# One transformer block on one core: conv taps and norm sums shared out anew, three norms' roots made with tokens on partitions, GpSimd closing part of the last norm

## The chip, the cores and the metric

The kernel runs as one program on one core of a Trainium2 chip. The metric is the device time of one execution in microseconds (us). The core has five instruction streams: TensorE (PE, with its weight loads shown apart as PEld), VectorE (DVE), ScalarE (ACT), GpSimd (POOL) and SyncE (SP), which here only issues DMAs.

## The reference

One block (DEPTH is 1) is applied to 1024 latent tokens of 1024 channels, all in float32. Context tokens and the DeltaNet layers of the full model don't enter at this depth. What is computed:

```python
mod = silu(c) @ w_mod + b_mod                 # six vectors: sh1 s1 g1 sh2 s2 g2
h = rms_norm(x, norm1_g) * (1 + s1) + sh1
u = h @ w_pw1 + b_pw1                         # 1024 -> 2048
u = a * sigmoid(gate)                         # the two halves of u
u = dwconv(u, w_dw) + b_dw                    # 31 taps, inside 16 segments of 64 tokens
u = silu(layer_norm(u, ln_g, ln_b))
x = x + g1 * (u @ w_pw2 + b_pw2)
h = rms_norm(x, norm2_g) * (1 + s2) + sh2
x = x + g2 * (relu(h @ w1) ** 2 @ w2)         # 1024 -> 4096 -> 1024
out = rms_norm(x, final_g)
```

## The kernel before

**Layout.** Channels lie on the 128 partitions in 8 chunks, tokens along the free dimension in two blocks of 512, A (`b` = 0) and B (`b` = 1). A tile `small` is 128x512, `big` 128x1024, `bank` one PSUM bank of 128x512.

**Products.** Every float32 product is three matmuls (`product`, lines 417 to 419): each operand is a rounded high part (an ACT cast) and the low remainder (a subtraction, line 366, on DVE or POOL), and hi·hi, hi·lo and lo·hi are summed. The second MLP product saves one block product in eight by sums and differences of blocks (`mlp_joint`, 7 of its groups `g`; matmuls at lines 838 to 840; the sums S of weights and T of hidden values are wide 128x1024 operations, also line 366). The eighth group, `mlp_apart`, forms its blocks directly, first for A, then for B.

**Stages.** Head: modulation vectors (`mod_chunk`, on DVE at line 516, or a POOL multiply at line 524 with an ACT sum at line 529) and the first norm of A. Then pointwise 1 with its gate, for A and B in the order of `PW1_ORDER`. Then the depthwise conv of A, its layer norm and pointwise 2, the second norm of A, and the first MLP product of A in 32 units (`up_first`). Block B's conv, layer norm, pointwise 2 and second norm are given out over those units: conv chunk c at unit `CONV_B[c]`, the layer norm at `LN_B`, pointwise 2 at `PW2_B`. Then the MLP of B, the eight groups, and the last norm (`finish`, line 912, and the output DMAs, line 919).

**Conv taps.** Of the 31 taps of a chunk one or two start the sums on ACT (line 598); `PE_TAPS` are matmuls with a diagonal matrix (line 616); `POOL_TAPS` are an ACT multiply (line 646) and a POOL add (line 651); the rest are DVE multiply-adds (line 661) into a PSUM bank. Lines 671 and 680 on DVE add the parts.

**Norm sums.** `Mean` takes eight chunks. The first 8 - `direct` are added up on an engine (line 366, POOL unless said), and the sum and each direct chunk go into PE (`feed`, line 438) as the moving operand of a matmul with a 128x128 matrix of 1/1024. This leaves the mean of each token in every partition of a bank. `rstd_of` makes the root over 128x512 on ACT (line 479) and its reciprocal on DVE (line 481). In a layer norm the mean is subtracted (line 695, DVE), squares are made (line 469, ACT), summed, and the result multiplied in (line 707, DVE), then silu (line 712), cast (line 359) and low part (line 366).

**Order.** All instructions are put in order before anything runs, by a list scheduler in the kernel (`Plan.run`): each operation has a cost in a table, an engine and a priority (the number given by `plan.at` plus its turn); on each engine the ready operation of smallest priority goes next, if tiles are free (`SLOTS`; `KEEP` holds back some for what comes soon, `CAPS` limits kinds of tiles). In this plan a POOL operation and a DVE operation marked `port` don't overlap. The order is then fixed, and an instruction that waits holds up everything behind it on its engine.

## Time and profile before

| | us |
|---|---|
| three runs | 1048.54, 1049.9, 1049.7 (median 1049.7) |
| profiled execution: its time / its span | 1048.54 / 1046.8 |
| PE busy | 979.6 (94%) |
| PE weight loads busy | 785.8 (75%) |
| DVE busy | 737.9 (70%) |
| POOL busy | 555.9 (53%) |
| ACT busy | 513.4 (49%) |
| first product starts / output DMAs of B are issued from | 23.25 / 1039.07 |
| mean granted TensorE clock | 0.982 |

A row of the timeline gives the start, the time, the engine, the line, the operation with its output and inputs and the number of instructions put together; in brackets the idle time just before it and who ended it. A group row gives the total busy time, the mean of one in ns, and the idle time before the group with its releasers. Single stages differ much from the average: DVE's busy share is near the whole for a long stretch and a third elsewhere.

### The profile page before, as it was taken

The page shows a single profiled execution, that of the slowest core. Times are in us where ns is not written, and L with a number is a line of the kernel's source. Part 1 is how long each engine was busy: PE and PEld are TensorE (multiplying, and loading weights), DVE is VectorE, ACT ScalarE, POOL GpSimd, SP SyncE. Part 2 cuts the span into 40 slices and gives each one's busy share as a digit, 9 for nine tenths or more (in the row PEclk, how much of TensorE's full clock was granted, in tenths as well). Part 3 has the DMA queues.
Part 4 walks back from the last instruction along what each step waited for, and adds up shares of the span by engine and source line. Part 5 has one row for each costly group of instructions (what it writes and reads, how often), then busy time and mean ns, then how long its engine had stood idle before and what let it go on. Part 6 is the DMA issues. An engine that isn't in the chain of part 4 may idle for free. (4 is left out here: it accounts for less than half of the span.)

```text
span 1046.8 us, 11616 instructions
## 1 busy us (share of the span) xinstructions
PE 979.6 (94%) x4164; PEld 785.8 (75%) x4164; DVE 737.9 (70%) x957; ACT 513.4 (49%) x757; POOL 555.9 (53%) x341
## 2 busy tenths in 40 slices
PE   1999999939999998999999999999999999999994
PEld 0877777618788886788788888888888888878783
DVE  6989999995399994623374666776767677575465
ACT  4476445787567873773363424343242524333222
POOL 0045678998978998661344244345344443632322
PEclk9999999969999998999999999999999999999998
DMA  9910213735415553554070411414131231303012
GB/s 359 402 72 1 81 41 124 259 110 175 178 66 186 171 178 105 181 182 159 21 280 2 138 64 44 138 61 141 40 122 59 77 119 47 121 1 121 0 50 111
DMA packets 52521, 125.26 MB, mean 120 GB/s; under 512 B 4464, under 2 KB 21104, under 8 KB 52464
## 3 DMA queue, kind: packets, MB, share of 16 engines
q1 hardware_dynamic: 52464, 124.53, 33.9%
q8 instruction: 32, 0.52, 0.2%
q14 instruction: 25, 0.20, 0.1%
HBM read 111.93 MB, written 12.58 MB: 119 GB/s over the span
## 5 line engine op out<-in xcount | busy, mean ns | idle before, releaser
L366 POOL TENSOR_TENSOR big<-big 128x1024 fp32r<-128x1024 f32 (+1 forms) x133 | 325.5, 2459 | 339.1 <-DVE big L366 218.6
L417 PE MATMUL bank<-big 128*128 128x512 f32 x896 | 358.2, 400 | 18.6 <-ACT big L359 11.1
L419 PE MATMUL bank<-big 128*128 128x512 f32 x896 | 351.1, 392 | 1.8 <-DVE big L366 1.8
L418 PE MATMUL bank<-big 128*128 128x512 f32 x896 | 351.6, 392 | 0.4 <-DVE big L501 0.3
L727 DVE SCALAR_TENSOR_TENSOR small<-bank,mod,small 128x512 f32<-128x512 f32 x228 | 170.5, 750 | 197.5 <-PE bank L840 144.4
L366 DVE TENSOR_TENSOR big<-big 128x1024 fp32r<-128x1024 f32 (+2 forms) x137 | 189.7, 1412 | 36.9 <-ACT big L379 18.5
L417 PEld LDWEIGHTS bank<-big 128*128 128x128 f32 x896 | 169.8, 190 | 59.8 <-ACT big L359 11.9
L661 DVE SCALAR_TENSOR_TENSOR bank<-small,vec,bank 128x472 f32<-128x472 f32 (+9 forms) x320 | 198.5, 694 | 3.1 <-ACT bank L598 2.2
L418 PEld LDWEIGHTS bank<-big 128*128 128x128 f32 x896 | 169.8, 189 | 40.6 <-issue 3.5
L419 PEld LDWEIGHTS bank<-big 128*128 128x128 f32 x896 | 169.7, 189 | 37.7 <-DVE big L366 2.2
L839 PE MATMUL bank<-big 128*128 128x512 f32 x456 | 178.2, 391 | 2.5 <-DVE big L366 2.4
L838 PE MATMUL bank<-big 128*128 128x512 f32 x456 | 177.9, 390 | 0.0
L840 PE MATMUL bank<-big 128*128 128x512 f32 x456 | 177.4, 389 | 0.0
L798 ACT CAST big<-big 128x1024 fp32r<-128x1024 f32 x106 | 106.1, 1045 | 93.1 <-POOL big L366 40.5
L651 POOL TENSOR_TENSOR small<-small 128x392 f32<-128x392 f32 (+3 forms) x104 | 110.0, 1075 | 28.0 <-ACT small L646 15.5
L379 ACT CAST big<-big 128x1024 fp32r<-128x1024 f32 x92 | 95.1, 1041 | 21.1 <-PE bank L840 11.4
L366 POOL TENSOR_TENSOR small<-small 128x512 f32<-128x512 f32 x44 | 57.0, 1295 | 90.8 <-ACT small L469 59.4
L839 PEld LDWEIGHTS bank<-big 128*128 128x128 f32 x456 | 85.6, 188 | 23.3 <-DVE big L366 5.4
L838 PEld LDWEIGHTS bank<-big 128*128 128x128 f32 x456 | 85.6, 188 | 18.2 <-issue 0.2
L840 PEld LDWEIGHTS bank<-big 128*128 128x128 f32 x456 | 85.6, 188 | 17.4
L786 ACT ACTIVATE small<-bank 128x512 f32<-128x512 f32 x32 | 19.2, 599 | 154.3 <-PE bank L419 154.3
L469 ACT ACTIVATE small<-small 128x512 f32<-128x512 f32 x64 | 38.3, 624 | 87.8 <-DVE small L727 85.2
(54 smaller groups left out, 628.0 us busy)
## 6 DMA issues: line engine op xcount, KB each, us to landing
big<-in_w SPq DMA_DIRECT2D x96, 512.0 KB, 3.8
big<-in_wmod SPq DMA_DIRECT2D x48, 512.0 KB, 5.3
big<-in_wpw SPq DMA_DIRECT2D x28, 512.0 KB, 5.0
hidden<-small SPq DMA_DIRECT2D x32, 256.0 KB, 2.4
big<-hidden SPq DMA_DIRECT2D x16, 512.0 KB, 4.6
small<-in_xA SPq DMA_DIRECT2D x16, 256.0 KB, 4.5
big<-in_wfirst SPq DMA_DIRECT2D x8, 512.0 KB, 10.2
small<-in_xB SPq DMA_DIRECT2D x16, 256.0 KB, 7.3
```

What stands on the lines that cost most here:

```text
L366: lambda: eng_of[o.eng].tensor_tensor(out=out(), in0=a(), in1=b(), op=op), r, w, part=part, port=port,
L379: plan.op("act", c_act(D), lambda: act.copy(t(wh), t(raw)), [raw], [wh], also=[wl])
L417: pe.matmul(o, wh, hi(a)[:, s], start=first, stop=False)
L418: pe.matmul(o, wh, lo(a)[:, s], start=False, stop=False)
L419: pe.matmul(o, wl, hi(a)[:, s], start=False, stop=last)
L651: return pool.tensor_tensor(out=dst, in0=dst, in1=seg(t(m))[:, :, tt], op=ALU.add)
L661: dve.scalar_tensor_tensor(out=dst, in0=src, scalar=w, in1=dst, op0=ALU.mult, op1=ALU.add)
L727: lambda s=s, p=p: dve.scalar_tensor_tensor(out=t(x)[:, s], in0=cut(s, p), scalar=scale.t, in1=t(x)[:, s], op0=ALU.mult, op1=ALU.add,),
L798: plan.op("act", c_act(D), lambda: act.copy(t(h), t(x)), [x], [h], also=[l])
L838: pe.matmul(t(p), t(wh)[:, cs], t(hh)[:, ns], start=first and k == 0, stop=False, skip_group_check=not first)
L839: pe.matmul(t(p), t(wh)[:, cs], t(hl)[:, ns], start=False, stop=False, skip_group_check=not first)
L840: pe.matmul(t(p), t(wl)[:, cs], t(hh)[:, ns], start=False, stop=k == 1, skip_group_check=not first)
```

## The change

- **Taps**: `POOL_TAPS` goes from 6 per chunk of A and 7 per chunk of B to uneven lists (46 and 62 in all, before 48 and 56). `PE_TAPS` of A goes from 32 to 25. What is left falls to DVE: 161 instead of 152 for A, 162 instead of 168 for B.
- **Order of stages**: pointwise 1 of B's chunks 0 and 1 comes third and fourth; the conv chunks of B start at units 0, 3, ..., 21 instead of 0, 2, ..., 14; its layer norm and pointwise 2 at unit 22 instead of 16 and 18.
- **Low parts and block sums**: B's first MLP product has its weights' low parts on POOL instead of DVE. In a joint group, three of the four S sums go from POOL to DVE, three of seven weight low parts from POOL to DVE and three of seven hidden low parts from DVE to POOL: DVE has 14 wide operations instead of 15, POOL 12 instead of 11.
- **Norm sums**: the conv mean of A feeds two chunks directly instead of one; A's layer norm feeds all eight squares into PE instead of five (no POOL adds); B's layer norm and second norm feed only the full sum.
- **Turned roots** (`TURNED`: first norm of A, second norm of B, last norm of B): the squares' chunk becomes the stationary operand and one column of the 1/1024 matrix the moving one, four 128x1 matmuls per feed (new line 451). The mean then has the tokens on the partitions, as 128x4. Root (506) and reciprocal (508) work on 128x4. A DVE operation (512) spreads the result over a 128x512 tile of diagonals, and one matmul with the 1/1024 matrix (521) brings it into all partitions. In the head an ACT copy (526) brings it to SBUF.
- **B's first norm** (`H1B_POOL`): ACT adds the shift in place, and casts in a second pass; the low part is a POOL subtraction instead of a DVE operation.
- **Last norm of B** (`FIN_POOL` = 3): for three chunks ACT multiplies by `final_g` ahead of time (963), copies the reciprocal root to SBUF (968), and POOL multiplies; DVE does the other five.
- **Scheduler**: `KEEP` 6 and 4 become 2 and 3; `CAPS` of tap tiles 3 becomes 4, of wave tiles 12 becomes 14. The identity matrix is loaded before `vec` instead of after the head.

New line numbers of what stays: 366 is 373, 438 is 446, 479 and 481 are 499 and 501, 661 is 713, 695 is 747, 707 is 759, 727 is 779, 912 is 976.

```diff
-POOL_TAPS = ((6,) * KC, (7,) * KC)
+POOL_TAPS = ((5, 8, 5, 10, 5, 4, 7, 2), (10, 7, 5, 7, 8, 7, 9, 9))
 PW1_ORDER = (
-    (0, 4), (0, 5), (0, 6), (0, 7), (1, 4), (1, 5), (1, 6), (1, 7), (1, 0), (1, 1),
+    (0, 4), (0, 5), (1, 0), (1, 1), (0, 6),
+    (0, 7), (1, 4), (1, 5), (1, 6), (1, 7),
 )
-CONV_B = (0, 2, 4, 6, 8, 10, 12, 14)
-LN_B, PW2_B = 16, 18
-PE_TAPS = ((4,) * KC, (0,) * KC)
+CONV_B = (0, 3, 6, 9, 12, 15, 18, 21)
+LN_B, PW2_B = 22, 22
+PE_TAPS = ((4, 2, 4, 4, 2, 2, 2, 5), (0, 0, 0, 0, 0, 0, 0, 0))
-UP_LO = ("pool", "dve")
-S_ENG, T_ENG = ("pool",) * 4, ("dve",) * 4
+UP_LO = ("pool", "pool")
+S_ENG, T_ENG = ("dve", "dve", "pool", "dve"), ("dve", "dve", "dve", "dve")
-WLO_ENG, HLO_ENG = ("pool",) * 7, ("dve",) * 7
+WLO_ENG, HLO_ENG = ("pool", "pool", "dve", "pool", "dve", "dve", "pool"), ("dve", "pool", "dve", "pool", "dve", "pool", "dve")
+CM = (2, 1)
+HEAD_DIRECT, LNA, LNB, N2B, FA = 0, 8, 0, 0, 1
+TURNED = (True, False, False, False, True, True)
+H1B_POOL = True
+FIN_POOL = 3
-KEEP = {"big": 6, "small": 4}
+KEEP = {"big": 2, "small": 3}
-CAPS = {"raw": 4, "head": 7, "w": 8, "tmp": 6, "tap": 3, "taps": 4, "acc": 8, "wave": 12}
+CAPS = {"raw": 4, "head": 7, "w": 8, "tmp": 6, "tap": 4, "taps": 4, "acc": 8, "wave": 14}
...
+            def emit_turned():
+                ((_, p),) = self.acc
+                for q in range(QT):
+                    pe.matmul(
+                        t(p)[:, q : q + 1], t(x)[:, q * P : (q + 1) * P], ones.t[:, 0:1],
+                        start=first and q == 0, stop=last, skip_group_check=True,
+                    )
...
+        root = Buf(None, None, const.tile([P, QT], F32, name="root"))
...
+            lambda: act.activation(root.t, t(p)[:, 0:QT], AF.Sqrt, bias=eps.t[:, 0:1]), [p, eps], [root], "sqrt",
...
+        plan.op("dve", 100, lambda: dve.reciprocal(root.t, root.t), [root], [root])
+        spread = small(mean.b)
...
+            lambda: dve.scalar_tensor_tensor(
+                out=t(spread).rearrange("p (q n) -> p q n", q=QT),
+                in0=ident.t.unsqueeze(1).to_broadcast([P, QT, P]), scalar=float(D),
+                in1=root.t.unsqueeze(2).to_broadcast([P, QT, P]), op0=ALU.mult, op1=ALU.mult,
+            ),
...
+            lambda: pe.matmul(t(p), ones.t, t(spread), start=True, stop=True), [ones, spread], [p],
...
+        if eng == "pool":
+            plan.op(
+                "act", c_act(TB[b], 1),
+                lambda: act.activation(t(y), t(y), AF.Identity, bias=shift.t), [y, shift], [y],
+            )
+            split_pair(b, "pool", out, y)
+            return out
...
-    vA = layer_norm(0, 5)
+    vA = layer_norm(0, LNA)
...
+            if j >= KC - n:
+                binary("pool", TB[b], ALU.mult, lambda x=x: t(x), lambda x=x: t(x), lambda: t(r), [x, r], [x])
```

**How the order moves, at two places.** First DVE at A's layer norm, from the middle of the stretch between the subtractions (695 or 747) and the reciprocal of the root. The `bank<-small,vec,bank` rows are taps of block B's first chunks, `sc` and `g1b` are columns of the modulation. Before:

```order
L1013 TENSOR_SCALAR g1b<-mod,vec 128x1
L661 SCALAR_TENSOR_TENSOR bank<-small,vec,bank 128x8x53
L661 SCALAR_TENSOR_TENSOR bank<-small,vec,bank 128x8x54 x2
L661 SCALAR_TENSOR_TENSOR bank<-small,vec,bank 128x8x55
L539 TENSOR_SCALAR sc_88<-mod,vec 128x1
L661 SCALAR_TENSOR_TENSOR bank<-small,vec,bank 128x8x55
L661 SCALAR_TENSOR_TENSOR bank<-small,vec,bank 128x8x56 x2
L661 SCALAR_TENSOR_TENSOR bank<-small,vec,bank 128x8x57 x2
L661 SCALAR_TENSOR_TENSOR bank<-small,vec,bank 128x8x58
L481 RECIPROCAL bank<-bank 128x512
L707 TENSOR_TENSOR small<-small,bank 128x512 x8
```

After, from the subtractions on:

```order
L747 TENSOR_TENSOR small<-small,bank 128x512 x8
L1077 TENSOR_SCALAR g1b<-mod,vec 128x1
L713 SCALAR_TENSOR_TENSOR bank<-small,vec,bank 128x8x59 x2
L713 SCALAR_TENSOR_TENSOR bank<-small,vec,bank 128x8x60
L591 TENSOR_SCALAR sc_88<-mod,vec 128x1
L713 SCALAR_TENSOR_TENSOR bank<-small,vec,bank 128x8x60
L713 SCALAR_TENSOR_TENSOR bank<-small,vec,bank 128x8x61 x2
L713 SCALAR_TENSOR_TENSOR bank<-small,vec,bank 128x8x62 x2
L501 RECIPROCAL bank<-bank 128x512
L759 TENSOR_TENSOR small<-small,bank 128x512 x7
```

Eight taps stand between the last subtraction and the reciprocal now; before it was 19, of which the fence shows the last ten.

Second, the end of the program on DVE, from the last norm of A. Line 727 (now 779) adds products into the residual, 912 (now 976) multiplies a chunk of the output. Before:

```order
L481 RECIPROCAL bank<-bank 128x512
L912 SCALAR_TENSOR_TENSOR small<-small,vec,bank 128x512 x8
L727 SCALAR_TENSOR_TENSOR small<-bank,mod,small 128x512 x8
L481 RECIPROCAL bank<-bank 128x512
L912 SCALAR_TENSOR_TENSOR small<-small,vec,bank 128x512 x8
```

and now:

```order
L501 RECIPROCAL bank<-bank 128x512
L976 SCALAR_TENSOR_TENSOR small<-small,vec,bank 128x512 x8
L779 SCALAR_TENSOR_TENSOR small<-bank,mod,small 128x512 x8
L508 RECIPROCAL root<-root 128x4
L512 SCALAR_TENSOR_TENSOR small<-ident,root 128x512
L976 SCALAR_TENSOR_TENSOR small<-small,vec,bank 128x512 x5
```

and on PE after the last product, now (before, two 128x512 matmuls of line 438 stood there):

```order
L890 MATMUL bank<-big 128x512
L891 MATMUL bank<-big 128x512
L892 MATMUL bank<-big 128x512
L451 MATMUL bank<-ones,small 128x1 x8
L521 MATMUL bank<-small,ones 128x512
```

The 128x512 reciprocal of B's last norm has gone, a small one and the spreading operation stand in its place, three of the eight closing multiplies have left DVE, and PE has eight 128x1 matmuls and one 128x512 in place of two 128x512.

More of the change, by code (lines that the diff above doesn't have):

```diff
@@ L71 @@
 class Op:
-    __slots__ = ("eng", "costs", "emit", "prio", "table", "deps", "bufs", "left", "ready", "end", "after", "lag", "port")
+    __slots__ = ("eng", "costs", "emit", "prio", "turn", "table", "deps", "bufs", "left", "ready", "end", "after", "lag", "port")
 class Plan:
@@ L128, in run @@
         events, seq, order = [], 0, []
-        waiting = sorted(self.ops, key=lambda o: o.prio, reverse=True)
+        waiting = sorted(self.ops, key=lambda o: o.turn, reverse=True)
         def push(o):
@@ L156, in run @@
                 waiting.pop()
-            near = waiting[-1].prio + NEAR if waiting else 0
+            near = waiting[-1].turn + NEAR if waiting else 0
             for e in engines:
@@ L176, in run @@
                                 caps[b.cap] = caps.get(b.cap, 0) + 1
-                    kept = KEEP if o.prio > near else {}
+                    kept = KEEP if o.turn > near else {}
                     if any(free[s] < n + kept.get(s, 0) for s, n in need.items()) or any(
@@ L475, in rstd_of @@
         ((_, p),) = mean.acc
-        r = p if in_bank else small(mean.b)
+        if not mean.turned:
+            r = p if in_bank else small(mean.b)
+            plan.op(
+                "act", c_act(TB[mean.b]),
+                lambda: act.activation(t(r), t(p), AF.Sqrt, bias=eps.t[:, 0:1]), [p, eps], [r], "sqrt",
+            )
+            plan.op("dve", 6.4 * TB[mean.b], lambda: dve.reciprocal(t(r), t(r)), [r], [r])
+            return r
+        root = Buf(None, None, const.tile([P, QT], F32, name="root"))
         plan.op(
-            "act", c_act(TB[mean.b]),
-            lambda: act.activation(t(r), t(p), AF.Sqrt, bias=eps.t[:, 0:1]), [p, eps], [r], "sqrt",
-        )
-        plan.op("dve", 6.4 * TB[mean.b], lambda: dve.reciprocal(t(r), t(r)), [r], [r])
+            "act", 200,
+            lambda: act.activation(root.t, t(p)[:, 0:QT], AF.Sqrt, bias=eps.t[:, 0:1]), [p, eps], [root], "sqrt",
+        )
+        plan.op("dve", 100, lambda: dve.reciprocal(root.t, root.t), [root], [root])
+        spread = small(mean.b)
+        plan.op(
+            "dve", c_stt(TB[mean.b]),
+            lambda: dve.scalar_tensor_tensor(
[3 more added lines that the diff above has]
+            ),
+            [ident, root], [spread], port=True,
+        )
+        plan.op(
+            "pe", 1.67 * TB[mean.b],
+            lambda: pe.matmul(t(p), ones.t, t(spread), start=True, stop=True), [ones, spread], [p],
+        )
+        if in_bank:
+            return p
+        r = small(mean.b)
+        plan.op("act", c_act(TB[mean.b]), lambda: act.copy(t(r), t(p)), [p], [r])
         return r
@@ L906, in finish @@
     def finish(b, xl, ms):
+        n = FIN_POOL if b else 0
+        for j in range(KC - n, KC):
+            plan.op(
+                "act", c_act(TB[b], 1),
+                lambda x=xl[j], j=j: act.activation(t(x), t(x), AF.Copy, scale=col(C_FG, j)), [xl[j], vec], [xl[j]],
+            )
         rstd = rstd_of(ms)
+        if n:
+            r = small(b)
+            plan.op("act", c_act(TB[b]), lambda: act.copy(t(r), t(rstd)), [rstd], [r])
         for j in range(KC):
             x = xl[j]
-            plan.op(
-                "dve", c_stt(TB[b]),
-                lambda x=x, j=j: dve.scalar_tensor_tensor(
-                    out=t(x), in0=t(x), scalar=col(C_FG, j), in1=t(rstd),
-                    op0=ALU.mult, op1=ALU.mult,
-                ),
-                [x, rstd, vec], [x], port=rstd.size != "bank",
-            )
+            if j >= KC - n:
+                binary("pool", TB[b], ALU.mult, lambda x=x: t(x), lambda x=x: t(x), lambda: t(r), [x, r], [x])
+            else:
+                plan.op(
+                    "dve", c_stt(TB[b]),
+                    lambda x=x, j=j: dve.scalar_tensor_tensor(
+                        out=t(x), in0=t(x), scalar=col(C_FG, j), in1=t(rstd),
+                        op0=ALU.mult, op1=ALU.mult,
+                    ),
+                    [x, rstd, vec], [x], port=rstd.size != "bank",
+                )
             plan.op(
@@ L946, in trunk @@
     xs0 = load_x(0)
+    load(ident, eye, P)
     load(vec, vecs, NVEC)
-    ms = Mean(0, 0, "dve")
+    ms = Mean(0, HEAD_DIRECT, "dve", TURNED[0])
     for k in range(KC):
@@ L970, in trunk @@
     plan.at(1010)
-    load(ident, eye, P, [h1[0][5]])
     xs1 = load_x(1, [h1[0][5]])
@@ L980, in trunk @@
         h1[1].append(
-            modulated(1, xs1[k], r1, sc1[k], mod[SH1][k], True)
+            modulated(1, xs1[k], r1, sc1[k], mod[SH1][k], True, "pool" if H1B_POOL else "dve")
         )
@@ L1059, in trunk @@
         up_part(0, i)
-    sums = Mean(0, 1), Mean(1, 1)
+    sums = Mean(0, FA), Mean(1, 1, turned=TURNED[5])
     for g in range(NQ):
```

26 lines of the change are left out of this document (16 added, 10 removed).

## The prediction

> **What bounds the kernel now.** I read PE's waits first, since PE is busy for 94% of the span. They come to some 39 us, nearly all of it waits for other engines' norm work. They are listed as engine, line, what was waited for, us in total, times, longest.
>
> ```profile
> PE bank L438 <- POOL small L366: 16.9, 5, 8.5
> PE bank L438 <- DVE small L366: 14.5, 1, 14.5
> PE bank L417 <- ACT big L359: 11.1, 1, 11.1
> PE bank L417 <- ACT big L497: 6.7, 1, 6.7
> PE bank L839 <- DVE big L366: 2.4, 5, 1.8
> PE bank L419 <- DVE big L366: 1.8, 1, 1.8
> ```
>
> The head has 14.5 + 6.7; A's layer norm 8.5 + 11.1; B's layer norm most of the rest of the first row; the joint groups 4.2. Next, busy time by stretches of 25 us (PE, PEld, DVE, ACT, POOL, then the granted clock, DMA):
>
> ```profile
> 100.00:125.00 25.00, 25.00 (x104) 19.15 (x103) 24.97 (x42) 13.29 (x27) 14.09 (x14) 1.00 0.20 64
> 150.00:175.00 25.00, 24.22 (x102) 18.67 (x101) 24.93 (x42) 11.87 (x22) 20.75 (x16) 1.00 0.22 76
> 175.00:200.00 25.00, 25.00 (x107) 19.67 (x106) 21.97 (x39) 16.72 (x30) 25.00 (x19) 1.00 0.76 277
> 200.00:225.00 25.00, 14.47 (x40) 7.83 (x38) 24.90 (x46) 20.45 (x41) 24.92 (x15) 0.80 0.28 91
> ```
>
> Until A's conv ends both PE and DVE are full; from 175 POOL is full too, and DVE at 22 to 25. So at A's layer norm a norm's own operations stand in queues that have no room. The timeline there:
>
> ```profile
> 204.41 0.69 DVE L680 TENSOR_TENSOR small<-bank,small 128x512 f32<-128x512 f32 x1
> 208.71 4.86 DVE L695 TENSOR_TENSOR small<-small,bank 128x512 f32<-128x512 f32 x8
> 213.98 1.13 ACT L469 ACTIVATE small<-small 128x512 f32<-128x512 f32 x2
> 212.84 2.69 POOL L366 TENSOR_TENSOR small<-small 128x512 f32<-128x512 f32 x2
> 215.58 7.41 PE L438 MATMUL bank<-small,ones 128*128 128x512 f32 x12 [8.52 <-POOL small L366]
> 224.98 0.66 ACT L479 ACTIVATE bank<-bank,eps 128x512 f32<-128x512 f32 x1
> 222.01 3.66 DVE L661 SCALAR_TENSOR_TENSOR bank<-small,vec,bank 128x440 f32<-128x440 f32 x6
> 225.67 3.37 DVE L481 RECIPROCAL bank<-bank 128x512 f32<-128x512 f32 x1
> 230.09 1.06 ACT L529 ACTIVATE big<-big 128x1024 f32<-128x1024 f32 x1 [1.31 <-POOL big L524]
> 234.07 0.79 PE L417 MATMUL bank<-big 128*128 128x512 f32 x1 [11.08 <-ACT big L359]
> ```
>
> The last conv sum ends at 205.1, and PE resumes 29 us later. The squares are done at 215.1, but PE's six feeds start only at 215.58, behind two POOL adds, and take 7.4 us, on a throttled clock (0.80 in that stretch).
>
> **A's conv (DVE).** The prices come from these rows (of a group: total, mean ns of one) and from the closing 8 multiplies in 5.36 us further down, 0.67 a piece back to back:
>
> ```profile
> L651 POOL TENSOR_TENSOR small<-small 128x392 f32<-128x392 f32 (+3 forms) x104 | 110.0, 1075 | 28.0 <-ACT small L646 15.5
> 17.29 3.35 DVE L481 RECIPROCAL small<-small 128x512 f32<-128x512 f32 x1 [0.23 <-ACT small L479]
> ```
>
> Up to A's first subtraction DVE loses eight low parts (-8 x 0.67 = -5.4) and the head's reciprocal (-3.35), and gains a spread (+0.67), a tiny reciprocal (0.2) and five taps at 0.61 (+3.1; six in 3.66 above): -4.8 of full DVE work. Not all of it counts. In the head DVE waits for data that the changed chain brings no sooner (below), and POOL gets eight subtractions of 1.35 (two in 2.69 above; +10.8, in 75 to 175, where the windows leave it 4 to 11 us free per 25) and hands over its taps later. I take the first subtraction 2.0 sooner, 206.7 (ends: 4.8 sooner; 2 later if POOL's taps become the last to come). Seven diagonal matmuls fewer save PE time that it then waits for DVE; they count nothing.
>
> **A's layer norm.** All squares go straight into PE, so a feed can follow each square, and the two POOL adds (2.69) leave the chain. Eight subtractions from 206.7 end at 211.6; the last square 1.5 later as before, 213.1; its feed 1.0; a table load 1.3 ahead of the root: 215.4 at best. ACT also has modulation sums (line 529) between the squares, which wait for POOL; before they cost the root some 2 us after the feeds, and I take 216.9. DVE's eight taps (5.2 with the columns) let the reciprocal start at 217.4, where 19 taps before gave 225.67. From root to PE it took 9.1 and keeps its 3.4 reciprocal: PE resumes at 225.9, **-8.2**. Ends: -10.5 (no wait of ACT) and -3 (ACT behind two further POOL multiplies at 2.4).
>
> **B's layer norm.** The rows of PE before:
>
> ```profile
> 405.57 2.08 PE L438 MATMUL bank<-small,ones 128*128 128x512 f32 x2 [4.91 <-POOL small L366]
> 406.66 1.42 PE L417 MATMUL bank<-big 128*128 128x512 f32 x1
> 411.06 0.40 PE L417 MATMUL bank<-big 128*128 128x512 f32 x1
> 431.48 1.98 PE L438 MATMUL bank<-small,ones 128*128 128x512 f32 x4 [0.80 <-POOL small L366]
> ```
>
> From 400.66 (405.57 less its 4.91) to 411.06 PE did a feed (0.9) and nine matmuls (0.23 each): 7.4 lost in idle and cold clock; 431.48 costs 1.2 more (0.80 and the slow first feed). Now 600 product matmuls stand between A's second norm and this mean instead of 507: 93 x 0.227 = 21.1 us of cover (the pitch from 220 in 49.85, the last row quoted of the joint groups). PE is there at 400.7 - 8.2 + 21.1 = 413.6. POOL's part was done at 405.5; 8.2 sooner, six more taps at 1.075 later, it is ready near 404. So this wait goes. The next one stays: the squares are all added on POOL (seven adds, 8.9, behind subtractions and squares) against 48 matmuls (10.9): some 2.5 with its cold start. **-6.0** (ends -8.6 and 0, where the conv chunks, now three units apart, arrive as late as PE).
>
> **Turned norms.** No row shows a 128x1 matmul. A float32 feed leaves two weight loads and two matmul records:
>
> ```profile
> L438 PEld LDWEIGHTS bank<-small,ones 128*128 128x128 f32 x44 | 8.9, 219 | 40.1 <-POOL small L366 19.4 <-DVE small L366 14.5 <-issue 4.9
> L438 PE MATMUL bank<-small,ones 128*128 128x512 f32 x44 | 25.6, 702 | 31.3 <-POOL small L366 16.9 <-DVE small L366 14.5
> ```
>
> By the loads alone a 128x1 matmul takes 2 x 0.22 = 0.44, 1.8 per feed; by the matmul records 1.4, 5.6 per feed. I take the loads, since the moving side has one column: 0.45. The Trainium skill ("TensorE: Matmul & The Clock Gate", "LDWEIGHTS (loading the stationary operand)") has the load depend on the stationary operand's columns alone, P/1.2 ns, 107 ns for 128; the rows here show 190 to 219, so the measured value stands. By the page the eight matmuls at the end would take an estimated 1.7 instead of 3.6, and the sum would be 1.9 lower.
>
> At the end, before:
>
> ```profile
> 1032.18 1.98 PE L438 MATMUL bank<-small,ones 128*128 128x512 f32 x4 [1.64 <-POOL small L366]
> 1034.20 0.66 ACT L479 ACTIVATE bank<-bank,eps 128x512 f32<-128x512 f32 x1 [2.15 <-PE bank L438]
> 1034.89 3.37 DVE L481 RECIPROCAL bank<-bank 128x512 f32<-128x512 f32 x1 [3.57 <-ACT bank L479]
> 1038.30 5.36 DVE L912 SCALAR_TENSOR_TENSOR small<-small,vec,bank 128x512 f32<-128x512 f32 x8
> 1039.07 4.94 SPq L919 DMA_DIRECT2D out<-small  x8
> ...
> L532 ACT ACTIVATE mod<-mod,vec 128x1 f32<-128x1 f32 x24 | 6.9, 286 | 0.3
> ```
>
> Counted from 1032.18: eight 128x1 matmuls 3.6, tiny root 0.3 (as ACT's other 128x1 operations), tiny reciprocal 0.3, spread 0.75, the 128x512 matmul 1.0, copy 0.65, three POOL multiplies 4.0 (DVE's five, 3.3, run beside them), the last DMA 3.15 as before, with 0.3 of hand-overs: 14.05 against 1046.8 - 1032.18 = 14.6. **-0.5** (ends -2.9 and +7, by the two prices). In the head the same chain (1.8 cold, 0.3, 0.2, 0.75, 2.08 cold, 0.65 = 5.8) replaces 2.08 + 0.69 + 3.35 = 6.1: nothing gained for PE, whose work there is behind DVE's in any case. The second norm of B lies beside A's remaining products; without enough of them its chain of some 6 us would show: **+0.5** (0 to +4).
>
> **Joint groups.** The longest stall, and DVE's wide operations alone and in a row:
>
> ```profile
> 919.01 1.22 DVE L366 TENSOR_TENSOR big<-big 128x1024 fp32r<-128x1024 f32 x1
> 927.60 8.99 DVE L366 TENSOR_TENSOR big<-big 128x1024 f32<-128x1024 f32 x6
> 927.19 2.40 POOL L366 TENSOR_TENSOR big<-big 128x1024 fp32r<-128x1024 f32 x1 [1.68 <-DVE big L366]
> 934.13 0.50 PE L419 MATMUL bank<-big 128*128 128x512 f32 x1 [1.78 <-DVE big L366]
> 985.17 0.50 PE L839 MATMUL bank<-big 128*128 128x512 f32 x1 [1.75 <-DVE big L366]
> ...
> 850.00:900.00 50.00, 49.85 (x220) 40.95 (x219) 35.66 (x38) 19.21 (x22) 19.11 (x9) 1.00 0.19 64
> ```
>
> One DVE operation less and one POOL operation more per group, both far from full here: I take **0** (-3.9 if both stalls go, +8 if each group gets one of 1.2).
>
> The sum: -8.2 - 6.0 - 0.5 + 0.5 = **-14.2** on the span of 1046.8, 1032.6. Outside the span this execution had 1.7 (1048.54), which gives 1034.3, so 1034; it is 1.2 under the median of 1049.7, and I leave it so.
>
> **Rivals.** *POOL becomes the bound at A's layer norm* (eight more subtractions, uneven taps, full from 175 on as shown): the gain there falls from 8.2 to about 2, 1040. For it: PE's and ACT's waits for POOL above; against: three POOL adds and two taps of A (6 us) leave the same stretch. *B's conv is late in spite of the cover* (POOL taps 56 to 62): -6 falls away, 1040. *A 128x1 matmul costs what a full one does* (1.4): the end is 7 later, 1041; for it the records of 0.59 at least, against it the loads. *Slower: DVE's block sums.* T and three S sums now form one chain on DVE per group. Six wide operations took 8.99, not 6 x 1.13, and the excess of 2.2 is about what was left of the POOL operation begun at 927.19 (2.0): one waits for the other. If in all seven groups PE waits for the chain and once more for a low part, each 1.9 as at 934 and 985, that is 27 less the 3.7 that exists, +23: 1057. From 2.5 us per group on it eats the whole gain. Against it: PE has no stall in 850 to 900 (as in each such stretch from 600 on), with DVE at 36 of 50. The Trainium skill ("SBUF — State Buffer", "SBUF: two separate sides") has DVE operations with two SBUF inputs and POOL operations lock each other out of a shared port in full; the rows agree (2.2 against 2.0).
>
> **Chances.** Forecast 0.53 (own range 1026 to 1040), POOL-bound norm 0.16, late conv of B 0.11, dear 128x1 matmuls 0.09, slower groups 0.11. A range of 1025 to 1046 leaves out the last and 0.05 below. A measurement of this kernel can tell 0.2%, 2.1 us: faster than 1047.6 hold the first four but for 0.03, 0.86; the same 0.05; slower 0.09.
>
> **What would show it.** Right: PE's wait at A's layer norm ends near 226 with its feeds spread over 207 to 216; no wait of PE at B's mean; the reciprocals of 3.4 gone from head and end; 128x1 matmuls near 0.45. Wrong: the root of A's layer norm later than 219 behind line 581 (was 529) waiting for POOL; PE waiting at B's mean; new waits of PE on wide operations between 560 and 1000; eight 128x1 matmuls over 6 us.

## The result and the profile after

The changed kernel takes 1033.11 us (median; 1031.8 to 1034.25), the kernel before 1049.12 beside it on the same chip: a ratio of 0.985 [0.983, 0.987]. The profiled execution took 1034.25 with a span of 1032.4, 14.4 less than the 1046.8 of before; 14.2 was predicted. The medians lie 16.0 apart: the execution profiled after the change is the slowest of its four, and the one profiled before the second fastest of its four.

PE's waits after (engine, line, what was waited for, us in total, times, longest):

```profile
PE bank L451 <- DVE small L373: 14.0, 1, 14.0
PE bank L424 <- ACT big L366: 8.6, 1, 8.6
PE bank L446 <- ACT small L488: 4.6, 2, 2.8
PE bank L891 <- POOL big L373: 3.4, 4, 1.6
...
PE bank L451 <- POOL small L373: 3.0, 1, 3.0
```

The row of 16.9 us in which PE waited for POOL in a norm has shrunk to 0.8 and the 3.0 at the end (1.64 there before), and the wait for ACT at A's layer norm is 8.6 instead of 11.1. New are 4.6 behind squares on ACT, and four waits of the joint groups, now for POOL.

To see where the 14.4 come from I divide the span at three points of PE's timeline: its restart behind A's layer norm, the first joint matmul, and the end of the last product (its start plus the 0.23 at which products follow each other).

| | PE restarts after A's norm | restart to joint groups | joint groups | last product to end | span |
|---|---|---|---|---|---|
| before | 234.07 | 325.5 | 470.8 | 16.4 | 1046.8 |
| after | 224.21 | 319.5 | 469.4 | 19.25 | 1032.4 |
| difference | -9.9 | -6.0 | -1.4 | +2.85 | -14.4 |

Both kernels run 1344 product matmuls in the second stretch. In profiles of kernels that have the same code there it lies between 317.9 and 319.6, and PE's restart between 224.2 and 225.6, so a difference of 1.5 us in one profile says little. (In the second stretch the longer profiles have a throttled clock for 3.41 us at A's second norm, and the shorter ones don't.)

The timeline after at A's layer norm (start, us, engine, line, operation; in brackets the idle time before and what ended it):

```profile
202.00 0.69 DVE L732 TENSOR_TENSOR small<-bank,small 128x512 f32<-128x512 f32 x1
207.11 4.86 DVE L747 TENSOR_TENSOR small<-small,bank 128x512 f32<-128x512 f32 x8
208.50 7.13 PE L446 MATMUL bank<-small,ones 128*128 128x512 f32 x16 [1.81 <-ACT small L488]
216.38 0.66 ACT L499 ACTIVATE bank<-bank,eps 128x512 f32<-128x512 f32 x1
217.17 3.35 DVE L501 RECIPROCAL bank<-bank 128x512 f32<-128x512 f32 x1
224.21 0.79 PE L424 MATMUL bank<-big 128*128 128x512 f32 x1 [8.57 <-ACT big L366]
```

The eight feeds run one behind each square from 208.50 to 215.6; before, six of them could start only at 215.58. The root follows 0.75 behind the last feed, and the reciprocal finds DVE free almost at once.

Further rows of PE after, at the first product, the second norm of A, the mean of B's layer norm, that norm's second sum, B's second norm, and a joint group:

```profile
21.85 0.80 PE L424 MATMUL bank<-big 128*128 128x512 f32 x1 [2.22 <-ACT big L549]
...
274.31 1.13 PE L446 MATMUL bank<-small,ones 128*128 128x512 f32 x2 [2.77 <-ACT small L488]
...
412.90 1.88 PE L446 MATMUL bank<-small,ones 128*128 128x512 f32 x4
...
426.47 1.12 PE L446 MATMUL bank<-small,ones 128*128 128x512 f32 x2 [0.78 <-POOL small L373]
...
513.81 0.95 PE L451 MATMUL bank<-ones,small 128*128 128x1 f32 x8
...
560.03 0.50 PE L891 MATMUL bank<-big 128*128 128x512 f32 x1 [1.65 <-POOL big L373]
```

At B's mean PE no longer waits; 0.78 is left behind it. The eight records at 513.81 are four 128x1 matmuls, 0.24 each at the full clock, without a wait.

The end of the program after, all engines, in order of time:

```profile
1006.04 2.72 DVE L779 SCALAR_TENSOR_TENSOR small<-bank,mod,small 128x512 f32<-128x512 f32 x4
1008.18 8.09 POOL L373 TENSOR_TENSOR small<-small 128x512 f32<-128x512 f32 x6 [14.43 <-ACT small L488]
1016.33 3.54 PE L451 MATMUL bank<-ones,small 128*128 128x1 f32 x16 [3.02 <-POOL small L373]
1019.90 0.26 ACT L506 ACTIVATE root<-bank,eps 128x4 f32<-128x4 f32 x1 [4.38 <-PE bank L451]
...
1021.25 2.05 PE L521 MATMUL bank<-small,ones 128*128 128x512 f32 x2 [1.38 <-DVE small L512]
1023.33 0.58 ACT L968 COPY small<-bank 128x512 f32<-128x512 f32 x1 [3.17 <-PE bank L521]
1023.95 3.38 DVE L976 SCALAR_TENSOR_TENSOR small<-small,vec,bank 128x512 f32<-128x512 f32 x5 [2.85 <-ACT small L968]
1023.99 3.71 POOL L373 TENSOR_TENSOR small<-small 128x512 f32<-128x512 f32 x3 [7.72 <-ACT small L968]
```

PE's last product ends at 1013.3, and POOL adds B's squares until 1016.27; only then can the 128x1 matmuls start. POOL began these adds at 1008.18, behind B's first four residual sums (line 779, 1006.04), which stood on DVE behind the eight closing multiplies of A.

Before, DVE had these operations in the same order, and PE waited only 1.64. What differs is where PE's sums for A's last norm stand. Before:

```profile
1009.58 1.88 PE L438 MATMUL bank<-small,ones 128*128 128x512 f32 x4
```

and after:

```profile
994.75 1.88 PE L446 MATMUL bank<-small,ones 128*128 128x512 f32 x4
```

Before, 84 product matmuls come behind this row, and now 72. So from here to the last product's end there are 18.4 us instead of 20.8, and A's closing multiplies, B's residual sums and POOL's adds, which all come behind A's norm, end 2.4 us later against PE's products. The last square was ready at 1014.8, before POOL's sum.

From the start of the 128x1 matmuls to the end it is 16.07 us, where the same way took 14.6 before.

### The profile page after: what moved, and what is told of

It is laid out like the page before. It is cut to its first block, busy times and chain, and to the rows that moved or that the text cites. A ratio compares the mean times of both kernels' runs of the same rounds, so it can differ in the third digit from the quotient of the medians.

```text
span 1032.4 us, 11676 instructions
## 1 busy us (share of the span) xinstructions
PE 977.8 (95%) x4182; PEld 786.8 (76%) x4182; DVE 687.4 (67%) x941; ACT 524.0 (51%) x767; POOL 597.9 (58%) x366
## 5 line engine op out<-in xcount | busy, mean ns | idle before, releaser
L373 POOL TENSOR_TENSOR big<-big 128x1024 fp32r<-128x1024 f32 (+1 forms) x144 | 351.0, 2454 | 303.3 <-DVE big L373 139.6
L779 DVE SCALAR_TENSOR_TENSOR small<-bank,mod,small 128x512 f32<-128x512 f32 x228 | 167.4, 747 | 215.3 <-PE bank L892 171.9
L713 DVE SCALAR_TENSOR_TENSOR bank<-small,vec,bank 128x432 f32<-128x432 f32 (+10 forms) x323 | 200.9, 694 | 2.4 <-ACT bank L650 1.5
L373 DVE TENSOR_TENSOR big<-big 128x1024 fp32r<-128x1024 f32 (+2 forms) x126 | 159.5, 1285 | 27.4 <-ACT big L386 12.5
L703 POOL TENSOR_TENSOR small<-small 128x392 f32<-128x392 f32 (+4 forms) x108 | 113.5, 1084 | 13.9 <-ACT small L698 9.7
L373 POOL TENSOR_TENSOR small<-small 128x512 f32<-128x512 f32 x46 | 59.7, 1301 | 93.6 <-ACT small L488 64.9
```

Of the source, the lines that this page charges most:

```text
L373: lambda: eng_of[o.eng].tensor_tensor(out=out(), in0=a(), in1=b(), op=op), r, w, part=part, port=port,
L703: return pool.tensor_tensor(out=dst, in0=dst, in1=seg(t(m))[:, :, tt], op=ALU.add)
L713: dve.scalar_tensor_tensor(out=dst, in0=src, scalar=w, in1=dst, op0=ALU.mult, op1=ALU.add)
L779: lambda s=s, p=p: dve.scalar_tensor_tensor(out=t(x)[:, s], in0=cut(s, p), scalar=scale.t, in1=t(x)[:, s], op0=ALU.mult, op1=ALU.add,),
```

## The experiments

All times are medians of several rounds; a ratio stands against the kernel before, run on the same chip. Beside the first four runs the kernel before took 1049.0, beside the others 1048.21, so that a difference of one of these others from the changed kernel's 1033.11 can be some 0.9 off.

### The end as it was, and the end with DVE alone

In the changed kernel, the root of B's last norm made in the wide form again, and all eight closing multiplies on DVE:

```diff
-TURNED = (True, False, False, False, True, True)
-FIN_POOL = 3
+TURNED = (True, False, False, False, True, False)
+FIN_POOL = 0
```

> The changed kernel with the old end alone: B's last norm has its root over 128x512 again (two 128x512 matmuls, root 0.66, reciprocal 3.37) and DVE multiplies all eight chunks; nothing ahead of the last product moves. Theory: the new end is the one place where the change loses; in its trace it takes 16.07 us from the start of the last sums' matmuls to the end, where the old kernel took 14.6 from the same point, because the eight 128x1 matmuls take 3.54 and the 128x512 matmul runs cold in 2.05, and GpSimd's last result reaches its DMA some 1 us later. So the old end should be 1.5 us faster than the changed kernel, span near 1030.9. Rival: the tiny root does save the 3.4 us reciprocal, and the loss at the end comes from sums that are late anyway; then this is 2 to 3 us slower, near 1035.

1033.34 (0.985 [0.984, 0.987]), where the changed kernel took 1033.11. Its timeline at the end:

```profile
1015.85 1.98 PE L446 MATMUL bank<-small,ones 128*128 128x512 f32 x4 [3.02 <-POOL small L373]
1018.57 3.37 DVE L501 RECIPROCAL bank<-bank 128x512 f32<-128x512 f32 x1 [4.94 <-ACT bank L499]
```

The wait of 3.02 stays, so it doesn't come from the turned root. From the row of 1015.85 to the end of the span it is 14.55 against 16.07: the profile has the wide form 1.5 ahead, the times have the two equal. That the turned end is worth 2 to 3 us is refuted; that it costs anything, the times don't show. What the 1.5 of the profiles is, the next run tells.

Second, only the three closing multiplies back on DVE (`FIN_POOL = 0`):

> The changed kernel without GpSimd's share of the last norm: the turned root stays, DVE multiplies all eight chunks, ScalarE's three early multiplies and its copy go. Theory: eight multiplies at 0.67 from the end of the spreading matmul (1023.3) end at 1028.7 and the last DMA 3.15 later, 1031.9, against 1032.4: 0.5 us faster, perhaps 1 more since ScalarE's three multiplies no longer stand between the last squares. Rival: GpSimd's three multiplies did take 2 us off the end; then the span is near 1034.

1033.24 (0.985 [0.984, 0.987]), no difference either. Its timeline:

```profile
1016.88 1.95 PE L451 MATMUL bank<-ones,small 128*128 128x1 f32 x16 [3.05 <-POOL small L373]
1020.21 2.05 PE L521 MATMUL bank<-small,ones 128*128 128x512 f32 x2 [1.39 <-DVE small L512]
1022.29 5.36 DVE L976 SCALAR_TENSOR_TENSOR small<-small,vec,bank 128x512 f32<-128x512 f32 x8 [2.23 <-PE bank L521]
```

DVE starts right behind the spreading matmul (it ends at 1022.26), without ACT's copy, and its last multiply ends 5.4 behind it; in the changed kernel the shared ones end 4.4 behind it (1027.70). That is 1.0 for sharing. But from the last multiply to the end of the span it is 3.15 here and 4.7 there: more than the 1.0 is given back. The changed kernel's last three output transfers, those of POOL's chunks, and what SyncE's queue waited for from 1020 on:

```profile
1027.78 1.41 SPq L983 DMA_DIRECT2D out<-small  x3
```

```profile
SPq L983 <- DVE small L976: 19.2, 5, 18.2
```

The queue issues the chunks in their order, and waited for DVE five times and for POOL never. POOL's first chunk was ready at 1025.3, but its transfer stood behind the five of DVE, the last of them issued at 1027.35; then the three went out one by one, the last at 1028.77.

And the eight 128x1 matmuls took 1.95 here, not 3.54, after the same wait. In the profiles with the changed kernel's own end, the stretch from the last product was 19.25 to 19.35 where they took 3.5, and 17.75 to 17.9 where they took 2 (all after the same wait): with the quick ones, this end is as long as the wide form's 17.7.

### Three of A's squares added on POOL again

```diff
-HEAD_DIRECT, LNA, LNB, N2B, FA = 0, 8, 0, 0, 1
+HEAD_DIRECT, LNA, LNB, N2B, FA = 0, 5, 0, 0, 1
```

> The changed kernel with five squares of A's layer norm fed directly and three added up on GpSimd, as before the change. Theory: the direct feeds are what moved the root forward (by 8.6 us in the trace): the two additions on GpSimd stand behind its modulation multiplies, and the order now has 16 taps and two additions ahead of the reciprocal instead of eight taps. PE then resumes after A's layer norm near 230 instead of 224.2 and the span is 5 to 6 us longer, 1037.5. Rival: A's layer norm is earlier because DVE's work before it became less and the taps were shared out anew; then PE resumes within 1.5 us of 224.2 and the span is within 1.5 of 1032.4.

1040.31 (0.991 [0.990, 0.993]), 7.2 slower than the changed kernel. Its rows of PE:

```profile
212.77 7.73 PE L446 MATMUL bank<-small,ones 128*128 128x512 f32 x12 [5.77 <-POOL small L373]
229.61 0.80 PE L424 MATMUL bank<-big 128*128 128x512 f32 x1 [9.11 <-ACT big L366]
234.62 0.80 PE L425 MATMUL bank<-big 128*128 128x512 f32 x1 [4.21 <-DVE big L373]
```

The feeds wait for POOL again, and PE restarts 5.4 later. Then it waits 4.21 for DVE, where the changed kernel waited 0.49: at A's second norm, 192 products on, PE is 9.1 later (279.59 against 270.51). The new direct feeds are thus worth more than half of the 9.9 at this place. The profiled execution, the fastest of its four, is 3.6 longer than the changed kernel's; the 7.2 is that of the medians.

### B's convolution packed as before

```diff
-CONV_B = (0, 3, 6, 9, 12, 15, 18, 21)
-LN_B, PW2_B = 22, 22
+CONV_B = (0, 2, 4, 6, 8, 10, 12, 14)
+LN_B, PW2_B = 16, 18
```

> The changed kernel with block B's conv chunks at units 0, 2, ..., 14, its layer norm at 16 and pointwise 2 at 18, as before the change. Theory: the later places gave B's conv and norm their cover; with the old ones PE waits again at B's mean and squares: 3 to 6 us longer, 1036 to 1038. Rival: B's stalls went for other reasons (fewer DVE low parts, more room for tiles, all squares summed on GpSimd), and the planner spreads B's work over the units in any case; then the span stays within 1.5 us of 1032.4.

1036.95 (0.988 [0.987, 0.990]), 3.8 slower than the changed kernel. The wait at B's mean is back, here at 389:

```profile
389.01 1.12 PE L446 MATMUL bank<-small,ones 128*128 128x512 f32 x2 [2.96 <-POOL small L373]
```

### Each of the two alone in the kernel before

All squares of A's layer norm fed to PE, in the kernel before:

```diff
-    vA = layer_norm(0, 5)
+    vA = layer_norm(0, 8)
```

> The kernel before with one edit: all eight squares of A's layer norm fed into PE, none added up on GpSimd. In its order nine taps stand between the last subtraction and the reciprocal, where 19 stood. Theory: this alone moves the root; undoing it in the changed kernel cost PE 5.4 us at the restart after A's layer norm. PE resumes near 228 instead of 234.1 and the span is some 6 us shorter, 1041. Rival: in the old kernel GpSimd and ScalarE are held by modulation work either way and the gain needs the new taps and the low parts moved to GpSimd: then PE resumes after 232 and the span is within 2 us of 1046.8.

1044.4 (0.996 [0.995, 0.997]): 3.8 faster than the kernel before, though PE restarts 7.8 sooner. Rows of PE:

```profile
209.85 8.72 PE L438 MATMUL bank<-small,ones 128*128 128x512 f32 x16 [3.12 <-ACT small L469]
226.27 0.79 PE L417 MATMUL bank<-big 128*128 128x512 f32 x1 [7.70 <-ACT big L359]
405.08 2.07 PE L438 MATMUL bank<-small,ones 128*128 128x512 f32 x2 [3.65 <-POOL small L366]
625.23 0.50 PE L419 MATMUL bank<-big 128*128 128x512 f32 x1 [1.48 <-DVE big L366]
```

The joint groups begin 7.15 sooner and then last 473.8 instead of 470.8, with 1.5 more of waits for DVE's wide operations (625.23 is one). Part of the gain is given back there; what the other half of the 3.0 is stays open. At B's mean PE still waits for POOL until 405.1, as it did until 405.6 before, but 543 products instead of 507 stand ahead of it now, so that nearly all of the gain is still there at the joint groups.

B's convolution spread out, in the kernel before:

```diff
-CONV_B = (0, 2, 4, 6, 8, 10, 12, 14)
-LN_B, PW2_B = 16, 18
+CONV_B = (0, 3, 6, 9, 12, 15, 18, 21)
+LN_B, PW2_B = 22, 22
```

> The kernel before with one edit: block B's conv chunks at units 0, 3, ..., 21, its layer norm and pointwise 2 at unit 22. In its order 594 product matmuls stand between A's second norm and B's mean instead of 507. Theory: the wait at B's mean (4.91 and a cold clock after it) goes, those at the squares stay: 5 to 7 us shorter, span 1041. Rival: the old taps keep B's conv as late as PE comes, and DVE's low parts of B's weights now collide with it: within 2 us of 1046.8.

1042.83 (0.995 [0.993, 0.996]), 5.4 faster than before. PE's rows at B's mean and at its second sum:

```profile
420.06 1.88 PE L438 MATMUL bank<-small,ones 128*128 128x512 f32 x4
...
432.27 1.98 PE L438 MATMUL bank<-small,ones 128*128 128x512 f32 x4 [0.79 <-POOL small L366]
```

The wait at the mean is gone, the stretch up to the joint groups is 8.1 shorter (317.4), and the joint groups are 1.3 longer. The two edits alone add up to 9.2 of the 16.0 by which the medians differ. They were not tried together without the rest.

### The joint groups' engines as before

```diff
-UP_LO = ("pool", "pool")
-S_ENG, T_ENG = ("dve", "dve", "pool", "dve"), ("dve", "dve", "dve", "dve")
+UP_LO = ("pool", "dve")
+S_ENG, T_ENG = ("pool",) * 4, ("dve",) * 4
-WLO_ENG, HLO_ENG = ("pool", "pool", "dve", "pool", "dve", "dve", "pool"), ("dve", "pool", "dve", "pool", "dve", "pool", "dve")
+WLO_ENG, HLO_ENG = ("pool",) * 7, ("dve",) * 7
```

> The changed kernel with the block sums and low parts of the second MLP product, and the low parts of B's first one, on the engines they had before. Theory: the new division is worth little: PE lost 3.4 us in four waits in the joint groups with it and 3.5 in two without, so the span is 0 to 2 us longer. Rival (the slower case of the prediction): the chain of sums on DVE costs PE time in the groups, and the old division is 2 us or more faster.

1039.53 (0.991 [0.990, 0.993]), 6.4 slower than the changed kernel. Its waits for POOL in the joint groups:

```profile
PE bank L892 <- POOL big L373: 7.5, 6, 1.5
```

PE busy from 560 to 1000 in the changed kernel (first row) and in this one:

```profile
560.00:1000.00 440.00, 438.23 (x1924) 360.69 (x1925) 265.83 (x293) 162.60 (x187) 202.31 (x86) 1.00 0.22 76
```

```profile
560.00:1000.00 440.00, 432.29 (x1895) 354.37 (x1894) 270.38 (x297) 160.32 (x184) 189.26 (x79) 1.00 0.22 77
```

5.9 us of PE are lost in this stretch. The new division is worth 6, where I had expected 0 to 2. But the kernel before, with these engines, loses only 1.4 more than the changed one in its joint groups. So it is not the engines alone: they do worse with the changed kernel's tile limits or order. The limits were tried next:

```diff
 (on top of the last edit)
-KEEP = {"big": 2, "small": 3}
+KEEP = {"big": 6, "small": 4}
-CAPS = {..., "tap": 4, ..., "wave": 14}
+CAPS = {..., "tap": 3, ..., "wave": 12}
```

> The changed kernel with the old engines for block sums and low parts, and the old limits on tiles as well (KEEP 6 and 4, tap 3, wave 12). With the engines alone put back, PE had a wait of 1.21 us in each group (on GpSimd) and the kernel was 6 us slower. Theory: the old engines suit the old limits; with 14 wave tiles and small reserves the planner starts sums earlier and sends GpSimd's low parts later, and with both undone the joint groups run as in the old kernel, without those waits: 3 to 6 us faster than with the engines alone, 1034 to 1036. Rival: the old engines themselves are what costs, whatever the limits: within 1.5 us of 1039.5.

1039.49 (0.992 [0.990, 0.993]), the same. The waits in the joint groups are others, for DVE now, and come to as much (7.4; the longest of three):

```profile
607.53 0.50 PE L891 MATMUL bank<-big 128*128 128x512 f32 x1 [3.85 <-DVE big L373]
```

The tile limits don't explain it. What in the changed order makes the old division dear stays open.

But the limits move the end. With the old ones 84 products stand behind PE's sums for A's last norm again, and the wait for POOL is that of before:

```profile
1020.99 2.84 PE L451 MATMUL bank<-ones,small 128*128 128x1 f32 x16 [1.64 <-POOL small L373]
```

With the new limits and all else alike, in the run just above it, it is 72 products and 3.06; every run with the old limits has 84, and every run with the new ones 72. The end from the last product is 17.2 here, 19.3 there. In the medians this doesn't show: they are equal.

### The even taps

```diff
-POOL_TAPS = ((5, 8, 5, 10, 5, 4, 7, 2), (10, 7, 5, 7, 8, 7, 9, 9))
+POOL_TAPS = ((6,) * KC, (7,) * KC)
-PE_TAPS = ((4, 2, 4, 4, 2, 2, 2, 5), (0, 0, 0, 0, 0, 0, 0, 0))
+PE_TAPS = ((4,) * KC, (0,) * KC)
```

This puts back the taps of both blocks, and A's on PE too.

> The changed kernel with the old even division of the conv taps (6 and 7 on GpSimd, 4 on PE for A). Theory: DVE has nine taps of A less (-5.5) and six of B more, PE seven diagonal matmuls more (+5.3), which stand in PE's queue where it waits for DVE anyway, GpSimd two taps of A more in a stretch where it is full. A's conv ends within 2 us of 202.6 and the span is 0 to 3 us longer. Rival: the uneven division is the main part of the gain at A's layer norm; then PE resumes there after 229 and the span is over 5 us longer.

1042.87 (0.995 [0.993, 0.996]), 9.8 slower than the changed kernel. From its timeline, POOL's last tap add of block A, DVE's last sum of A's convolution, and PE's restart:

```profile
205.72 1.06 POOL L703 TENSOR_TENSOR small<-small 128x408 f32<-128x408 f32 x1
...
212.19 0.69 DVE L732 TENSOR_TENSOR small<-bank,small 128x512 f32<-128x512 f32 x1
...
231.90 0.79 PE L424 MATMUL bank<-big 128*128 128x512 f32 x1 [6.47 <-ACT big L366]
```

A's convolution ends at 212.9, in the changed kernel at 202.7. A's last chunk has six adds on POOL here, one by one between wide operations of 2.4 us, and the last ends at 206.8; with two adds, as in the changed kernel, they end at 192.3. DVE's last sum of A then stands behind taps of block B that were put ahead of it on DVE. To see whether the even taps fail only beside the low parts of B's first norm, which the change gave to POOL in the same stretch, those were put back on DVE as well:

```diff
 (on top of the last edit)
-H1B_POOL = True
+H1B_POOL = False
```

> The changed kernel with two parts undone together: the even division of taps, and the low parts of B's first norm on DVE. With the taps alone undone, PE resumed 7.7 us later after A's layer norm, at 231.9, and A's conv ended 9 us later. Theory now: the uneven taps are needed because GpSimd got those low parts; with eight subtractions more and its old taps GpSimd is what A's conv waits for, and the planner fills DVE with block B's taps (27 of them ahead of A's last sum instead of 4). With both undone A's conv ends near 205 as in the old kernel and PE resumes near 226.5, where the old kernel with eight direct squares alone resumed; the span is near 1035. Rival: the even taps are worse by themselves, whoever makes the low parts; then PE resumes after 230 and the span stays near 1041.8.

1041.74 (0.993 [0.992, 0.995]): hardly better. DVE's last sum of A's convolution starts at 212.86, and PE restarts later still:

```profile
233.41 0.80 PE L424 MATMUL bank<-big 128*128 128x512 f32 x1 [7.29 <-ACT big L366]
```

So the even taps are bad in the changed order by themselves. In the kernel before they weren't: its last sum was at 204.41. With the even taps alone put back, PE waits another 3.92 for DVE right behind its restart, so that at A's second norm it is as late as in the kernel before (282.1 against 281.2). The changed order brings A's last two chunks later (`PW1_ORDER` has block B's first two units ahead of them), which would explain why the last chunk must be light on POOL. That was not tried and is only argued.

### A better end

In the changed kernel DVE does A's eight closing multiplies ahead of B's first four residual sums, as the kernel before did, and POOL's six adds come late for it. Here the residual sums go first, two of B's last squares go straight into PE instead of one, and the root is wide:

```diff
+            plan.at(2950 + 10 * b)
             done(b)
+            plan.at(2920)
-    sums = Mean(0, FA), Mean(1, 1, turned=TURNED[5])
+    sums = Mean(0, FA), Mean(1, 2)
-FIN_POOL = 3
+FIN_POOL = 0
```

> A new version: the changed kernel with a new end. B's residual sums go ahead of A's closing multiplies on DVE, two squares of B are fed directly instead of one, B's root is over 128x512 as in the old kernel and DVE closes all chunks. Theory: at the end GpSimd's six additions form a chain that ends 3.1 us after the last product, since B's first four sums waited on DVE behind A's closing. With them first the chain is done when the last square is, at 1014.8 in the trace of the changed kernel; last feed 1.0, root 0.7, reciprocal 3.4, eight multiplies 5.4, last DMA 3.1: end at 1028.5, 4 us under the changed kernel. Rival: the order on DVE was not what held the sums; the end moves less than 1.5 us.

1029.87 (0.983 [0.981, 0.984]), 3.2 faster than the changed kernel, whose fastest run (1031.8) is above this one's slowest (1030.75). Measured from the kernel before, each beside its own runs, it is 2.3 (18.3 against 16.0). The end in its timeline:

```profile
1010.54 2.66 POOL L373 TENSOR_TENSOR small<-small 128x512 f32<-128x512 f32 x2 [3.81 <-ACT small L488]
1013.25 2.84 PE L446 MATMUL bank<-small,ones 128*128 128x512 f32 x6 [0.29 <-POOL small L373]
1016.83 3.37 DVE L501 RECIPROCAL bank<-bank 128x512 f32<-128x512 f32 x1 [3.08 <-ACT bank L499]
```

POOL is done at 1013.2, and PE waits 0.29 for it, not 3.02. From the last product to the end it is 15.9, where the changed kernel took 19.25 and its wide form in the first experiment 17.7. The same with the turned root (`Mean(1, 2, turned=TURNED[5])`):

> The same new end with the turned root. Its cost follows the clock: the eight 128x1 matmuls took 3.54 us in some runs and 1.95 in others, in which PE's clock was still up. Theory: with sums that come without a gap PE stays at full clock: the last feed 1.0, root 0.3, reciprocal 0.2, spread 0.7, matmul 1.0 and hand-overs 0.4 give 3.6 from the last square to the closing multiplies, where the wide root takes 5.1: 1.5 us faster than the wide version. Rival: PE's clock falls after the last product in any case; then the matmuls take 1.8 and 2.05 and the two versions are within 0.7 us of each other.

1029.8 (0.982 [0.981, 0.984]), the same as the wide one, where 1.5 less was expected. Its end:

```profile
1011.58 3.14 PE L451 MATMUL bank<-ones,small 128*128 128x1 f32 x24 [0.29 <-POOL small L373]
```

Both beat the changed kernel and the one before. What helps is the order on DVE and the shorter chain on POOL, which were changed together, so that their shares are not known; turning the root does nothing here. These runs keep the 72 products behind A's sums.

## Why the prediction was right, and where it wasn't

The predicted 1034 stands beside 1033.1, and the two largest terms came out where they were put. The size is in part luck: four terms were off and cancelled. The listed waits of PE add up to 53.4, not to 39 (which leaves out the head's 14.5); no term hangs on it.

**A's layer norm, -8.2 predicted, -9.9 measured.** Step by step: first subtraction 206.7 predicted, 207.11 measured; root 216.9 and 216.38; reciprocal 217.4 and 217.17; PE 225.9 and 224.21. The mechanism is shown by the run with five direct squares (+5.4 at PE's restart) and by the eight direct squares in the kernel before (-7.8). What was mis-sized is the last part: from root to PE it took 7.8, not the 9.1 of before, in which ACT waited 1.31 for POOL (row of 230.09) and now doesn't. The reciprocal was put at 217.4, a little before a root of 0.66 from 216.9 can end. What the prediction saw too little is how much the uneven taps belong to this term: with even taps all of the gain but 2 us is gone at the restart (231.9), and the rest at A's second norm. In the kernel before, the direct feeds gave 7.8 with even taps; so the two are not shares that add up. It had the taps as a count of operations, and not the question of what the last chunk waits for.

**B's layer norm, -6.0 predicted, -6.0 measured** between PE's restart and the joint groups. That the two are equal is luck: the stretch also holds B's second norm (+0.5) and A's second norm, and in other profiles of the same code it is up to 1.6 shorter. PE came to the mean at 412.90, predicted 413.6, without a wait. The second wait stayed, 0.78 and a cold start. The packed convolution in the changed kernel brought a wait of 2.96 back, the spread one in the kernel before took 8.1 off the stretch. One wait was not foreseen: 2.77 at A's second norm (274.31), against 0.98 before.

**B's second norm, +0.5.** It cost nothing: the chain lay wholly beside other work (PE came to it at 513.81 without a wait).

**The head, nothing.** The first product came at 21.85 instead of 23.25. What of these 1.4 reaches the end was not tried. Nor were the turned roots of the head and of B's second norm undone alone, or the low parts of B's first norm.

**Joint groups, 0 predicted, -1.4 measured.** DVE's block sums did not become the bound; the slower rival is refuted. (The existing waits that its +23 takes off are 4.2 by the rows, not 3.7.) Yet the term was right only as a net: against the old division inside this order the new one is worth 6, against the kernel before hardly more than two profiles differ by. I had read DVE's and POOL's load (36 and 19 us of 50), which says little: with the old division PE waits 7.5 for POOL while POOL is busy for 189 of 440. That it hangs on when an operation's turn comes is the likely reading, not shown.

**The end, -0.5 predicted, +2.85 measured: the step that failed.** The wait ahead of the sums and the way behind them were both too long. I took the wait for the sum of squares as before (1.64); it was 3.02. B's residual sums stand behind A's closing multiplies on DVE in both kernels. What moved is A's last norm, with 72 products behind its sums instead of 84, and with it all that stands behind. It is the tile limits that move it: with the old engines of the joint groups, the old limits bring 84 and 1.64 back where the new ones have 72 and 3.06. I had listed the limits among the changes and had no term for them. The order on DVE has its part in it: with the residual sums first and one square more fed directly, the wait is 0.29 with 72 products too. The spreading matmul took 2.05, not 1.0: it comes 1.38 after the last 128x1 matmul, on a throttled clock (0.50). From the last result (1027.70) to the end it took 4.7, not 3.15: POOL's three transfers stand in the queue behind DVE's five, and the last is issued 1.1 behind the last multiply. The price of a 128x1 matmul was right at the throttled clock: 3.54 for eight where 3.6 was said. That too is in part luck. It was worked out as two loads of 0.22 one after the other, a mean over both clocks; the loads overlap, and at the full clock eight took 1.95. The lower end of this term's range, -2.9, follows from neither of its two prices.

Of the rivals, POOL as the bound at A's norm, a late convolution of B and the dear 128x1 matmuls (over 6 us) are all refuted by the rows above.

## What to carry to other kernels

Ask of each operation in a changed order who waits for it: an engine's load told nothing of the joint groups or of the end here; at the end its place in the queue did. Ask it too when only a limit of the scheduler changes, for a limit moves the order far from where it was set: here it took 12 products from behind A's last norm. A gain at one stage need not reach the end whole: of 7.8 at A's norm, alone in the kernel before, 3.8 did. And before a norm is made cheaper at the end of a program, see whether its inputs are the later ones: sooner inputs gave 2 to 3 us, two forms of the root gave none.

## What the runs showed of the hardware

**The price of small matmuls after a pause depends on whether the clock has fallen by then.** After the same wait of 3.02 to 3.06 us the eight 128x1 matmuls at the end took 3.54 to 3.57 in four profiles and 1.95 to 2.09 in three; with a full clock four took 0.95. Over them the granted clock (third number from the end) was 0.50 in the changed kernel (first row) and 1.00 with DVE alone closing (second):

```profile
1016.40:1019.80 3.40, 3.40 (x16) 3.38 (x16) 0.00 (x0) 0.00 (x0) 0.00 (x0) 0.50 0.00 0
```

```profile
1016.90:1018.80 1.90, 1.90 (x16) 1.84 (x16) 0.00 (x0) 0.00 (x0) 0.00 (x0) 1.00 0.00 0
```

The Trainium skill ("TensorE: Matmul & The Clock Gate", "What's actually happening") says that the clock is gated by a free-running window of about 3.4 us, so that it is a matter of phase when a pause throttles it; these runs agree with it. In all fourteen traces the throttled stretches inside the program last 3.41, 6.83, 10.24 or 13.65 us, whole multiples of 3.41. There is one profile of each kernel, so that it is chance within one kernel is not shown.

**A float32 128x1 matmul takes as long as its two weight loads**: 0.24 us at the full clock and 0.44 at the throttled one. The sixteen loads of eight such matmuls were busy for 1.86 of the 1.95 and 3.45 of the 3.54 us. One load lasts 191 ns in the mean at the full clock and 328 at the throttled one, but the loads overlap, so that two cost less than twice that.

**Output transfers leave in the queue's order, not in that of the results**: the first chunk of POOL was ready at 1025.3 and its transfer was issued at 1027.78, behind the five of DVE. The three that came last were issued 0.5 us apart, and the end of the span came 4.7 behind the last multiply instead of 3.15. Whether another order of the chunks gives this back was not tried.
